# Attention's value products for two query blocks at a time, and the last down products in PSUM banks of their own

## The chip, the core and the metric

The kernel runs on one core of a Trainium2 chip. Five engines work side by side and meet only through semaphores: TensorE (PE in the profile, with its weight loads shown apart as PEld), VectorE (DVE), ScalarE (ACT), GpSimd (POOL) and SyncE (SP), which here issues nearly all DMA transfers. [...] The metric is the device time of one launch in microseconds; less is better. A time is given as the median of several runs.

## The reference

The reference is one transformer block in fp32 over 1024 tokens of width 1024, one batch row, one layer:

```
mod = silu(c) @ w_ada + b_ada            # sh1 sc1 g1 sh2 sc2 g2
h = rmsnorm(x) * (1 + sc1) + sh1
q_a k_a v_a | q_d k_d v_d z b a = split(h @ w_in)
y_attn  = dilated attention, 8 heads of 64, softmax over three dilated branches
y_delta = gated delta rule, 8 heads of 64, chunks of 64, short convolution
x = x + g1 * (concat(y_attn, y_delta) @ w_out)
h = rmsnorm(x) * (1 + sc2) + sh2
x = x + g2 * ((silu(h @ w_gate) * (h @ w_up)) @ w_down)      # d_ff = 2816
out = rmsnorm(x) * final_norm_g
```

The three dilated branches are one causal softmax over all 1024 keys: a bias table holds the log of how many branches contain a distance, and distances in no branch are masked.

## The kernel before

**Precision.** Products that need fp32 accuracy are made of three fp32r products: each operand is cut into a high part (an ACT cast) and a low part (a DVE or POOL subtraction), and high x high, high x low, low x high are summed in one PSUM bank. Attention's transposes (`L1332`) and value products (`L1349`) are plain fp32 instead; TensorE executes each plain fp32 value product as two recorded matmuls with a weight load each.

**Order of the work.** The build function writes the program in one order. A list scheduler then fixes the order on each engine: it plays the program against modelled durations and gives a free engine the ready instruction of the highest priority. Priority is the place in the program; `urgent()` moves what it encloses 6000 places forward, which in attention and in the down products is ahead of everything else in sight. `tc.issue_after(ins)` makes what it encloses follow `ins` on that engine. A tile of a pool with `bufs=n` waits until one of n buffers has been released by its last reader. `FILL` and `ahead()` place filler products (`L590`: input projections, later products with `w_out`) between the small products of delta rule and attention.

**Attention (`attend`, about 495 to 670 us).** A unit is one pair of heads `hp` (4 of them) and one block `qb` of 128 queries (8 of them). At step i of 32 units the program holds the scores of unit i (`att_score`: S products on PE, a DVE reduction to X, an ACT exponential, a POOL scaling), the transposes of unit i-1 (`att_turn`: per head one or two banks of up to four 128x128 transposes, copied by ACT for the first four key blocks and by DVE for the rest into a tile `et`), and the value products of unit i-3 (`att_value`). There are 4 `et` buffers, two per unit. `att_value` runs over the key blocks kb = 0..qb and in each over both heads e; head e takes 64 columns of `va` as weights, so its product uses half the columns of the PE array and lands in half the partitions of one bank `y`. Four query blocks share that bank, one after another; after the fourth, ACT copies it (`yh`, L1360) and DVE takes the rest (`yl`, L1361). A unit has 2(qb+1) value products.

**Down products (`down`, from 1186 us to the end).** The FFN's second half is done by a seven-product (Strassen-like) scheme: token half l, output half s, seven passes i over f = 0..10. Per f, two tiles of 128x512 are loaded by SP (`raw_load`: `da` activations, `db` weights; 6 buffers `wr`), cut by ACT and DVE (`parts`, 5 buffers each for `wh` and `wl`, urgent), and used in 12 matmuls: four token blocks b, each into a bank of its own, three products each. Passes 0, 1, 4 and 6 sum in the four banks X, pass 2 in Y, passes 3 and 5 in Z (Y's banks). After a pass its four banks are finished by `ends`, which the next pass calls at f = 1, 3, 5, 7: a copy, or `sum_end`: add, multiply by g2, add x, an ACT square whose accumulator gives the row sum; a row that is complete goes through `row_out`: an add, a square root, a reciprocal, two scalings and two stores.

The last pass (`down(6, ..., final=True)`) multiplies f = 0..6 for all four blocks, and keeps the parts of f = 7..10 (TAIL = 4) in 8 extra buffers; then each block b gets its 12 last products and is finished at once, so that only block 3 is left at the end:

```python
            if final:
                for f in range(n, NF):
                    down_mm(bank, b, pr[f], f, first)
                with urgent():
                    final[b]()
```

There `final[b]()` is L1835 (bank times g2), L1836 (plus x), L1838 (square), L1844 (sum of the two halves), L1845 (root), L1846 (reciprocal), L1851 on ACT and L1853 on DVE (the two halves scaled), L1856 (stores).

## Time and profile before

| | |
|---|---|
| time, median of 3 runs | 1403.61 us (1403.61 to 1405.59) |
| the profiled execution's own time | 1406.77 us |
| its span, first to last instruction | 1404.7 us |
| PE busy | 1349.1 us, 96% |
| DVE / ACT / POOL busy | 876.6 / 662.6 / 287.1 us |
| granted TensorE clock, mean | 0.992 |
| DMA moved | 245.68 MB, mean 175 GB/s |

In a list of instructions in order of time, a row is: start, duration, engine, line, operation, what is written from what, shape, and how many equal neighbours are merged (x32); a bracket at its end tells idle time before it and what ended that. Matmuls are pipelined: a 128x512 matmul is shown 0.39 us long, but the next starts 0.23 us later. In a table of stretches, each engine has its busy time and in brackets its number of instructions, then come the clock, the DMA engines' busy share and GB/s. A row of a group has minimum, median and maximum duration in ns.

### The profile page before, as it was taken

Reading aid. Unit: us, or ns where it says so; the run is one execution under the profiler, and the core shown is the slowest. Engines: PE = TensorE matmul, PEld = TensorE weight load, DVE = VectorE, ACT = ScalarE, POOL = GpSimd, SP = SyncE. Lnnn points to the kernel's source line nnn. Section 1 sums busy time; section 2 is a strip of 40 time slices with the busy share of each in tenths; the row PEclk is TensorE's granted clock in tenths of the full one; section 3 lists DMA queues with packets and bytes.
Section 4 is the critical chain, followed back from the end, with each engine's and each line's share of the span. In section 5 each row is a group of like instructions: output and inputs, shape, how many; then the busy total and the mean of one; then the engine's idle time right before and its main releaser. Section 6 shows DMA issues by size and latency. Waiting matters only on the chain.

```text
span 1404.7 us, 24467 instructions
## 1 busy us (share of the span) xinstructions
PE 1349.1 (96%) x8984; PEld 1110.7 (79%) x8984; DVE 876.6 (62%) x1669; ACT 662.6 (47%) x1287; POOL 287.1 (20%) x267
## 2 busy tenths in 40 slices
PE   8998999998999899999999999999999999999997
PEld 4778877887888677777877878888888888888886
DVE  3688484556835433666228987667575776474487
ACT  4498424356234355766147733333333333444446
POOL 2346412344213344543162000000000000000000
PEclk9999999999999999999999999999999999999999
DMA  8666565486352445521584345545363665765566
GB/s 307 229 190 167 162 209 167 130 248 180 119 151 68 129 128 169 184 91 54 169 263 161 120 158 169 175 147 176 130 207 106 210 207 186 259 222 197 194 221 238
DMA packets 169872, 245.68 MB, mean 175 GB/s; under 512 B 32566, under 2 KB 73831, under 8 KB 169752
## 3 DMA queue, kind: packets, MB, share of 16 engines
q1 hardware_dynamic: 169752, 244.12, 53.8%
q8 instruction: 71, 1.16, 0.3%
q14 instruction: 49, 0.40, 0.1%
HBM read 181.30 MB, written 67.48 MB: 177 GB/s over the span
## 4 chain that ended last, share of the span: by engine, by line
PE 56%; DMA 4%; DVE 3%; ACT 2%; issue 1%; POOL 1%; SPq 0%; DVEq 0%; ACTq 0%; POOLq 0%
PE wua L1591 9%; PE wga L1591 8%; PE X L1786 6%; PE wuc L1591 4%; PE wgc L1591 4%; PE Z L1786 4%; PE g_a L590 3%; PE wo L590 3%; PE y L1349 3%; PE wgb L1591 2%; PE Y L1786 2%; PE wub L1591 2%; PE tr L1332 2%; PE S L1308 1%; PE S L1309 1%
## 5 line engine op out<-in xcount | busy, mean ns | idle before, releaser
L1581 DVE TENSOR_TENSOR wl_db<-wr_db,wh_db 128x512 fp32r<-128x512 f32 x77 | 53.1, 691 | 74.7 <-ACT wh_db L1580 74.6
L1580 ACT CAST wh_db<-wr_db 128x512 fp32r<-128x512 f32 x77 | 47.9, 622 | 96.5 <-PE X L1786 41.3
L1312 DVE CUSTOM_DVE_ANT_0 X<-S,ng 128x512 f32<-128x512 f32 (+3 forms) x64 | 36.8, 586 | 55.4 <-PE S L1309 39.8
L1786 PE MATMUL X<-wh_db,wl_da 128*128 128x512 f32 x176 | 68.5, 389 | 0.0
L1786 PE MATMUL X<-wh_db,wh_da 128*128 128x512 f32 x176 | 68.5, 389 | 0.0
L1786 PE MATMUL X<-wl_db,wh_da 128*128 128x512 f32 x176 | 68.5, 389 | 0.0
L1317 ACT ACTIVATE X<-X,sc 128x128 f32<-128x128 f32 (+7 forms) x64 | 49.4, 773 | 36.9 <-DVE sc L1312 33.5
L1319 POOL TENSOR_SCALAR X<-X,sc 128x128 f32<-128x128 f32 (+7 forms) x64 | 50.5, 792 | 75.1 <-DVE sc L1318 70.7
L1581 DVE TENSOR_TENSOR wl_da<-wr_da,wh_da 128x512 fp32r<-128x512 f32 x77 | 52.8, 685 | 2.0 <-ACT wh_da L1580 2.0
L590 PE MATMUL g_a<-hh,wh_a 128*128 128x512 f32 x128 | 53.1, 415 | 0.0
L590 PE MATMUL wo<-yh,wh_wo 128*128 128x512 f32 x128 | 51.6, 406 | 1.0 <-DVE xo L1400 1.0
L590 PE MATMUL wo<-yl,wh_wo 128*128 128x512 f32 x128 | 50.6, 395 | 0.9 <-DVE yl L1411 0.9
L590 PE MATMUL g_a<-hh,wl_a 128*128 128x512 f32 x128 | 51.2, 400 | 0.0
L590 PE MATMUL wo<-yh,wl_wo 128*128 128x512 f32 x128 | 51.2, 400 | 0.0
L590 PE MATMUL g_a<-hl,wh_a 128*128 128x512 f32 x128 | 51.1, 399 | 0.0
L1580 ACT CAST wh_da<-wr_da 128x512 fp32r<-128x512 f32 x77 | 47.4, 616 | 6.8 <-PE wua L1591 5.8
L1580 ACT CAST wh_wg_s<-wg_s 128x512 fp32r<-128x512 f32 x33 | 20.6, 623 | 57.3 <-PE wuc L1591 24.6
L1332 PE MATMUL tr<-ident,X 128*128 128x128 f32 x288 | 44.7, 280 | 2.8 <-DVE et L1335 1.7
L231 POOL TENSOR_TENSOR wl_wo<-wr_wo,wh_wo 128x512 fp32r<-128x512 f32 x24 | 32.9, 1375 | 61.2 <-ACT wh_wo L230 55.9
L1349 PE MATMUL y<-et,va 128*64 128x128 f32 x576 | 43.5, 281 | 0.3 <-DVE yl L1361 0.3
L1332 PEld LDWEIGHTS tr<-ident,X 128*128 128x128 f32 x288 | 34.0, 142 | 12.2 <-issue 4.3
L1580 ACT CAST wh_wu_s<-wu_s 128x512 fp32r<-128x512 f32 x33 | 20.4, 621 | 43.8 <-PE wga L1591 17.2
(544 smaller groups left out, 4324.2 us busy)
## 6 DMA issues: line engine op xcount, KB each, us to landing
wm<-in_wada SPq DMA_DIRECT2D x44, 512.0 KB, 6.6
wr_da<-ao_d SPq DMA_DIRECT2D x77, 256.0 KB, 3.0
wr_wu<-in_wu SPq DMA_DIRECT2D x50, 256.0 KB, 2.7
wr_wg<-in_wg SPq DMA_DIRECT2D x48, 256.0 KB, 2.8
ao_d<-a SPq DMA_DIRECT2D x44, 256.0 KB, 2.5
wr_wd<-in_wdn SPq DMA_DIRECT2D x44, 256.0 KB, 3.1
wr_db<-wt_d SPq DMA_DIRECT2D x44, 256.0 KB, 2.7
ao_d<-as SPq DMA_DIRECT2D x33, 256.0 KB, 2.0
```

Source lines behind the costliest of these rows:

```text
L231: (eng or nc.gpsimd).tensor_tensor(out=lo[:, :n], in0=raw[:, :n], in1=hi[:, :n].bitcast(F32), op=ALU.subtract)
L590: last[0] = nc.tensor.matmul(ps, a[:, w0], b[k0 + k4][:, cs], start=(i == 0), stop=(i == n - 1))
L1308: nc.tensor.matmul(ps[:, 0 : c1 - c0], QS[:, qs], KS[:, c0:c1], start=True, stop=False)
L1312: nc.vector.tensor_tensor_reduce(out=X[:, c0:c1], in0=ps[:, 0 : c1 - c0], in1=ng[:, u + c0 : u + c1], scale=1.0, scalar=(3e38 if m is None ...
L1317: nc.scalar.activation(X[:, 0:nk], X[:, 0:nk], AF.Exp, scale=-1.0, bias=m, accum_out=sc[:, 2:3])
L1319: nc.gpsimd.tensor_scalar(out=X[:, 0:nk], in0=X[:, 0:nk], scalar1=sc[:, 3:4], scalar2=0.0, op0=ALU.mult, op1=ALU.add)
L1332: nc.tensor.transpose(ps[:, (kb - c0) * P : (kb - c0 + 1) * P], X[:, kb * P : kb * P + P], ident)
L1349: nc.tensor.matmul(yps[64 * e : 64 * e + 64, yc], va[:, kb, 64 * e : 64 * e + 64], ets[e][:, kb, :], start=(kb == 0), stop=(kb == qb),)
L1580: nc.scalar.copy(hi, src)
L1581: (eng or nc.vector).tensor_tensor(out=lo, in0=src, in1=hi.bitcast(F32), op=ALU.subtract)
L1591: nc.tensor.matmul(ps, a[:, w0], b, start=(first and k == 0 and n_ == 0), stop=(k == 3 and n_ == 2), skip_group_check=True,)
L1786: nc.tensor.matmul(bank[b], a[:, ts_], w, start=(first and f == 0 and n_ == 0), stop=(f == NF - 1 and n_ == 2), skip_group_check=True,)
```

## The change

In attention, `att_value` is called for odd `qb` only, and does the products of qb and qb-1 together. They are urgent, and ordered: first two products of head 1 of block qb (for qb < 7 with key blocks 0 and qb, for 7 with 7 and 0), then, after the second of these on PE, all the others. The bank `y` is taken at the first of the two groups. The `et` buffers go from 4 to 6.

In the down products, the tiles of f = 7..10 of the last pass are loaded and cut during pass 5 (at f = 1, 3, 5, 7), their weights first multiplied by g2 on DVE; their products go into four banks W of their own (Z's banks, free after pass 5's ends). So X of the last pass is complete after f = 6, and `last_end` does X times g2 plus x while the W products run; per block there is then one add, the square and `row_out`. In `row_out` the sum of the two halves is no longer an instruction: the square is scaled to give means, eps is added to the first half's mean where that half is finished, and the root takes that sum as its bias.

```diff
-XB, ETB, AT, AV = 5, 4, 1, 3
+XB, ETB, AT, AV = 5, 6, 1, 3
...
-        if qb % 4 == 0:
+        if qb % 4 == 1:
             ybanks[hp] = ybank(f"y{hp}_{qb}")
         yps = ybanks[hp]
...
+        seq = {q: (0, *range(q, 0, -1)) if q < 7 else (q, *range(q)) for q in (qb - 1, qb)}
+        parts = [(q, kb, e) for q in (qb, qb - 1) for kb in seq[q] for e in (1, 0)]
+        parts[1:2], parts[2:3] = parts[2:3], parts[1:2]
+        mm = None
+        with turn(f"y{hp}_{qb}"), urgent():
+            for i, (q, kb, e) in enumerate(parts):
+                with tc.issue_after(mm.ins) if i else ExitStack():
+                    ins = nc.tensor.matmul(
+                        yps[64 * e : 64 * e + 64, (q % 4) * P : (q % 4 + 1) * P],
+                        va[:, kb, 64 * e : 64 * e + 64], ets[q % 2][e][:, kb, :],
+                        start=(kb == seq[q][0]), stop=(kb == seq[q][-1]),
                     )
+                mm = ins if i < 2 else mm
...
-            if i >= AV:
+            if i >= AV and units[i - AV][1] % 2:
                 hp, qb = units[i - AV]
-                att_value(hp, qb, ets.pop(i - AV))
+                att_value(hp, qb, [ets.pop(i - AV - 1), ets.pop(i - AV)])
...
         b = raw_load(wdn_src(i, f), f"db{i}_{f}")
+        if p is not None:
+            with urgent():
+                nc.vector.tensor_tensor(out=b, in0=b, in1=g2r[:, dsl[0]], op=ALU.mult)
         return parts(a, f"da{i}_{f}", p=p), parts(b, f"db{i}_{f}", p=p)
...
-        n = NF - TAIL if final else NF
-        for f in range(NF):
-            pr[f] = down_parts(i, f, pz if f >= n else None)
...
+        n = NF - TAIL if tail else NF
+        for f in range(n):
+            pr[f] = down_parts(i, f)
+            for b in range(4):
+                down_mm(bank, b, pr[f], f, first and f == 0, f == n - 1)
+            if i == 5 and f % 2 == 1 and len(held) < TAIL:
+                t = NF - TAIL + len(held)
+                held[t] = down_parts(6, t, pz)
             if f % 2 == 1 and ends:
                 ends.pop(0)()
...
-                    down_mm(bank, b, pr[f], f, first)
+                    down_mm(tail, b, held[f], f, f == n, f == NF - 1)
                 with urgent():
-                    final[b]()
+                    last[b]()
...
-        sq = pz.tile([P, HALF], F32, name=f"sq3_{l}{s}{b}", tag="sq3", bufs=2)
-        nc.scalar.activation(sq, t, AF.Square, accum_out=rn[:, 4 * l + b, s : s + 1])
+        square(l, s, b, t)
         if s == l:
+            r = rn[:, 4 * l + b]
+            nc.vector.tensor_tensor(out=r[:, 2:3], in0=r[:, s : s + 1], in1=eps1, op=ALU.add)
...
-        nc.vector.tensor_tensor(out=r[:, 2:3], in0=r[:, 0:1], in1=r[:, 1:2], op=ALU.add)
-        nc.scalar.activation(r[:, 2:3], r[:, 2:3], AF.Sqrt, bias=eps1, scale=1.0 / D)
-        nc.vector.reciprocal(r[:, 3:4], r[:, 2:3])
+        nc.scalar.activation(r[:, 3:4], r[:, 1 - l : 2 - l], AF.Sqrt, bias=r[:, 2:3])
+        nc.vector.reciprocal(r[:, 3:4], r[:, 3:4])
...
+    def last_end(src, more):
+
+        def at(b):
+            x = x_in(1, 0, b)
+            t = y[1, 0][b]
+            nc.vector.tensor_tensor(out=t, in0=src[b], in1=g2r[:, dsl[0]], op=ALU.mult)
+            nc.vector.tensor_tensor(out=t, in0=t, in1=x, op=ALU.add)
+
+            def go():
+                nc.vector.tensor_tensor(out=t, in0=more[b], in1=t, op=ALU.add)
+                square(1, 0, b, t)
+                row_out(1, b)
...
-    down(6, X, False, sum_end(1, 0, X, None, True), final=True)
+    W = four("W")
+    down(6, X, False, last_end(X, W), tail=W)
```

More of the change, by code (lines that the diff above doesn't have):

```diff
@@ L1341, in att_value @@
         va = loaded[hp][0]
-        if qb % 4 == 0:
+        if qb % 4 == 1:
             ybanks[hp] = ybank(f"y{hp}_{qb}")
         yps = ybanks[hp]
-        yc = slice((qb % 4) * P, (qb % 4 + 1) * P)
-        with turn(f"y{hp}_{qb}"):
-            for kb in range(qb + 1):
-                for e in range(2):
-                    nc.tensor.matmul(
-                        yps[64 * e : 64 * e + 64, yc], va[:, kb, 64 * e : 64 * e + 64], ets[e][:, kb, :],
-                        start=(kb == 0), stop=(kb == qb),
+        seq = {q: (0, *range(q, 0, -1)) if q < 7 else (q, *range(q)) for q in (qb - 1, qb)}
[9 more added lines that the diff above has]
+                        start=(kb == seq[q][0]), stop=(kb == seq[q][-1]),
                     )
+                mm = ins if i < 2 else mm
         if qb % 4 == 3:
@@ L1770, in build @@
     nc.sync.dma_start(gfr, I["gfin"].to_broadcast([P, D]))
+    dsl = [slice(s * HALF, (s + 1) * HALF) for s in range(2)]
     def wdn_src(i, f):
@@ L1779, in down_parts, with down_mm @@
         b = raw_load(wdn_src(i, f), f"db{i}_{f}")
+        if p is not None:
+            with urgent():
+                nc.vector.tensor_tensor(out=b, in0=b, in1=g2r[:, dsl[0]], op=ALU.mult)
         return parts(a, f"da{i}_{f}", p=p), parts(b, f"db{i}_{f}", p=p)
-    def down_mm(bank, b, pr, f, first):
+    def down_mm(bank, b, pr, f, first, last):
         (ah, al_), (wh, wl) = pr
@@ L1786, in down_mm, with down @@
             nc.tensor.matmul(
-                bank[b], a[:, ts_], w, start=(first and f == 0 and n_ == 0), stop=(f == NF - 1 and n_ == 2),
-                skip_group_check=True,
+                bank[b], a[:, ts_], w, start=(first and n_ == 0), stop=(last and n_ == 2), skip_group_check=True,
             )
     ends = []
-    def down(i, bank, first, end, final=False):
+    held = {}
+    def down(i, bank, first, end, tail=None):
         pr = {}
-        n = NF - TAIL if final else NF
-        for f in range(NF):
-            pr[f] = down_parts(i, f, pz if f >= n else None)
-            if f < n:
-                for b in range(4):
-                    down_mm(bank, b, pr[f], f, first)
+        n = NF - TAIL if tail else NF
[6 more added lines that the diff above has]
+                held[t] = down_parts(6, t, pz)
             if f % 2 == 1 and ends:
                 ends.pop(0)()
-        assert not ends
-        if final:
+        while ends:
+            ends.pop(0)()
+        if tail:
             with urgent():
-                final = [end(b) for b in range(4)]
+                last = [end(b) for b in range(4)]
         for b in range(4):
-            if final:
+            if tail:
                 for f in range(n, NF):
-                    down_mm(bank, b, pr[f], f, first)
+                    down_mm(tail, b, held[f], f, f == n, f == NF - 1)
                 with urgent():
-                    final[b]()
+                    last[b]()
             else:
@@ L1824, in build @@
     rn = pz.tile([P, 8, 4], F32, name="rn", tag="rn")
-    dsl = [slice(s * HALF, (s + 1) * HALF) for s in range(2)]
-    xr = {}
     def x_in(l, s, b):
@@ L1831, in x_in, with square @@
         return x
+    def square(l, s, b, t):
+        sq = pz.tile([P, HALF], F32, name=f"sq3_{l}{s}{b}", tag="sq3", bufs=2)
+        nc.scalar.activation(sq, t, AF.Square, scale=1.0 / 32, accum_out=rn[:, 4 * l + b, s : s + 1])
     def half_end(l, s, b, src, t, x):
@@ L1856, in row_out @@
             nc.sync.dma_start(out[tb * P : (tb + 1) * P, dsl[s]], t)
+    def last_end(src, more):
[8 more added lines that the diff above has]
+                row_out(1, b)
+            return go
+        return at
     def copy_end(dst, src):
@@ L1868, in go @@
                 t = y[l, s][b]
-                if other is not None:
-                    add(t, src[b], other[b])
-                half_end(l, s, b, src[b] if other is None else t, t, x)
+                add(t, src[b], other[b])
+                half_end(l, s, b, t, t, x)
                 if row:
```

## The prediction

> **What bounds the kernel now.** I read the page first (busy shares), then tables of stretches around the two places that change, then PE's instructions in order of time there, then what PE waited for in attention, and last the end of the DVE and ACT lists.

> ```profile
> span 1404.7 us, 24467 instructions
> PE 1349.1 (96%) x8984; PEld 1110.7 (79%) x8984; DVE 876.6 (62%) x1669; ACT 662.6 (47%) x1287; POOL 287.1 (20%) x267
> ...
> 573.00:637.00 64.00, 60.68 (x478) 46.71 (x477) 45.14 (x135) 44.28 (x94) 31.63 (x30) 0.97 0.40 126
> ...
> 1336.08:1357.84 21.76, 21.76 (x97) 18.02 (x97) 18.75 (x31) 11.62 (x25) 0.00 (x0) 1.00 0.74 242
> 1357.84:1366.00 8.16, 8.16 (x37) 6.76 (x37) 4.85 (x8) 3.43 (x7) 0.00 (x0) 1.00 0.62 186
> 1366.00:1396.00 30.00, 29.92 (x132) 24.43 (x131) 26.29 (x53) 21.50 (x44) 0.00 (x0) 1.00 0.72 251
> ```

> PE is the bound: 96% over the whole, 95% in the middle of attention (60.68 of 64.00 us), without a gap in the last two down passes. In the stretches the columns after the length are PE, PEld, DVE, ACT, POOL, clock, DMA share, GB/s. Whatever PE needs less in attention the whole program ends earlier, since the products behind wait for PE too; after PE's last matmul only the end chain counts.

> **Attention: what one group of value products costs.** PE's list between 498.84 and 669.28 us holds 45 unbroken groups of `y` products where 32 units ask for 32; the first and last, and five stretches that give prices:

> ```profile
> 498.84 0.44 PE L1349 MATMUL y<-et,va 128*64 128x128 f32 x4
> ...
> 609.21 0.40 PE L1308 MATMUL S<-KS,QS 128*128 128x512 f32 x1
> 609.44 0.39 PE L1309 MATMUL S<-KL,QS 128*128 128x512 f32 x1
> 609.76 0.43 PE L1349 MATMUL y<-et,va 128*64 128x128 f32 x2
> 610.12 0.39 PE L1308 MATMUL S<-KS,QS 128*128 128x256 f32 x1
> ...
> 637.31 1.97 PE L1349 MATMUL y<-et,va 128*64 128x128 f32 x32
> 639.21 0.50 PE L1308 MATMUL S<-KS,QS 128*128 128x512 f32 x1
> 639.55 0.40 PE L1309 MATMUL S<-KL,QS 128*128 128x512 f32 x1
> 639.78 0.39 PE L1308 MATMUL S<-KS,QS 128*128 128x512 f32 x1
> ...
> 641.50 0.44 PE L1349 MATMUL y<-et,va 128*64 128x128 f32 x4
> 641.86 0.33 PE L1308 MATMUL S<-KS,QS 128*128 128x128 f32 x1
> ...
> 666.29 3.05 PE L1349 MATMUL y<-et,va 128*64 128x128 f32 x50
> ```

> From start to the next start: 32 records take 1.90 us, 4 take 0.36, so 0.055 a record and 0.14 fixed. Before a group, S to `y` takes 0.32 where S to S takes 0.23: 0.09. After it, S to S takes 0.34 (639.21 to 639.55) where the next takes 0.23: 0.11. A group costs 0.34 us beside its records. Two records (one product) take 0.36, as long as four: a product without a partner in the other half of the array loses 0.10, and 18 of the 45 groups have an odd number of products.

> The change asks for 16 groups. Their first products wait for the head whose copies come last, and the rest follows, so they should stay whole. Step by step:
> - 29 groups fewer at 0.34: -9.9 us; 18 odd ends at 0.10: -1.8.
> - The new head of a group puts two products of head 1 and then two of head 0 in a row, so pairs in opposite halves begin two records late: two steps of 0.11 (two records each), 0.22 us. Bounds 0 and 0.22; I take 0.22, since the lone two records above were not filled up either: 16 x 0.22 = +3.5.
> - For qb = 5 the first two products wait for two different copies (ACT's and DVE's). If the first goes alone, four groups split: 4 x 0.34 = +1.4; bounds 0 and 1.4, and I take 1.4, because the x2 group above is just such a lone first product.
> - `et` from 4 to 6 buffers, `y`'s bank taken one unit later, the filler 0.64 of `y0_0` without a taker: nothing on PE. The cover is that PE has S, transposes or filler to do; if it is gone, the copies' wait below is what PE sees.
> Sum: -6.8 us; ends -11.7 (no loss at the head, no split) and -1.0 (half the groups broken up as now).

> [...]

> What could now wait is the head of each group: it is urgent, so it stands in PE's order as soon as the planned copy ends, and everything behind it on PE (S, transposes, filler) waits with it.

> ```profile
> PE tr L1332 <- DVE et L1335: 1.7, 3, 0.8
> PE y L1349 <- DVE yl L1361: 0.3, 1, 0.3
> ...
> L1337 ACT COPY et<-tr x60: 267/565/606, 500.4 to 666.0; 128x512 f32<-128x512 f32 x40, 128x384 f32<-128x384 f32 x8, 128x128 f32<-128x128 f32 x6, 128x256 f32<-128x256 f32 x6
> ```

> These are PE's waits (total us, times, longest) and the copy. `y` waited once, for its bank, and never for a copy, though the broken groups show that products were often placed right at a copy's end. Bounds 0 and one copy, 0.565, per group (9.0 us). I take 0.

> **Down: what moves into pass 5.** For four f: 8 loads of 256 KB by SP, 8 casts on ACT, 8 subtractions and 4 new multiplications on DVE, from pass 6 into the first eight f of pass 5. DVE's price is 18.75 us / 31 = 0.605 each, so 12 x 0.605 = 7.3 us. The first eight f then ask DVE for 26.0 us in 21.76. Of it only subtractions and held work are urgent: 28 x 0.605 = 16.9 us, which fits. The 16 steps of pass 4's ends (9.7 us) get 4.8 there and need 4.9 in the last three f, where six subtractions of 8.16 us leave 4.5: they end 0.4 us into pass 6. Block 3's bank X, which an end must have read, is wanted 3 x 0.68 = 2.0 us into pass 6 (three blocks of three matmuls at 0.227). So PE doesn't wait, with 1.6 us to spare.

> The loads: 22 of pass 5, 4 of `x`, 8 moved; 28 fall into the first eight f, 7.3 MB in 21.8 us.

> ```profile
> 1344.24:1346.96 2.72, 2.72 (x13) 2.25 (x13) 2.72 (x5) 1.21 (x3) 0.00 (x0) 1.00 0.85 257
> ...
> 1379.50:1382.20 2.70, 2.70 (x14) 2.23 (x13) 2.70 (x6) 2.68 (x6) 0.00 (x0) 1.00 0.94 335
> ```

> At the first row's rate (257/0.85 = 302 GB/s when full) they take 24.3 us, 2.5 too long; at the second's (356 GB/s) 20.6, in time. SP sends them in order through the 6 `wr` buffers, and a late held tile stops the DVE and ACT work queued behind it. In these rows DVE was full and PE lost nothing, with three f of loads in hand. Bounds 0 and +2.5; I take +0.3, nearer to the row that shows the same pile-up in pass 6. [...]

> In pass 6, DVE loses 8 x 0.605 of its 26.29 us. The banks W are free when pass 5's ends have read Z, more than 10 us before PE asks for them. Eight tiny additions of eps go into passes 2 and 4, under their matmuls. PE's 924 matmuls stay.

> **The end.** Now, for block 3, DVE and ACT:

> ```profile
> 1395.54 0.39 PE L1786 MATMUL X<-wh_db,wl_da 128*128 128x512 f32 x1
> ...
> 1386.66 0.68 DVE L1836 TENSOR_TENSOR y<-y,xr 128x512 f32<-128x512 f32 x1
> 1388.92 0.75 DVE L1853 SCALAR_TENSOR_TENSOR y<-y,rn,gfr 128x512 f32<-128x512 f32 x1
> ...
> 1396.64 0.68 DVE L1835 TENSOR_TENSOR y<-X,g2r 128x512 f32<-128x512 f32 x1
> 1397.65 0.69 DVE L1836 TENSOR_TENSOR y<-y,xr 128x512 f32<-128x512 f32 x1
> 1399.19 0.16 DVE L1844 TENSOR_TENSOR rn<-rn 128x1 f32<-128x1 f32 x1
> 1400.19 0.75 DVE L1853 SCALAR_TENSOR_TENSOR y<-y,rn,gfr 128x512 f32<-128x512 f32 x1
> ```

> PE ends at 1395.93. The last scaling starts 4.26 us later, behind a multiplication, an addition, root and reciprocal that are also mixed with block 2's. The row of an undisturbed block (addition 1386.66, scaling 1388.92) needs 2.26 us from addition to scaling. After the change one addition is left in front and L1844's step is gone. With it at 1396.0 the scaling starts by 1398.3 at the latest undisturbed (-1.9), or 0.6 later behind block 2's scaling; without L1844, 0.3 earlier. So -1.9, ends -1.3 and -2.2. The stores behind keep their 3.8 us to 1404.7.

> **Sum.** -6.8 + 0.3 - 1.9 = -8.4 us. The profiled execution has a span of 1404.7 and a time of 1406.77; it becomes 1396.3 and 1398.4. The median of the runs is 1403.61, so 1395.2.

> **Rivals.**
> - *Slower: each group waits at its head.* Place: PE before the 16 groups. Price: a copy of 0.565 and about 0.2 of hand-over (my estimate from the gaps of the end chain, 0.2 to 0.4 between engines), 0.77 x 16 = 12.2 us: 1407.4. It decides from 8.4/16 = 0.53 us per group. For: urgent leaves no slack, and S, transposes and filler stand behind it. Against: `y` waited 0.3 us in all. Chance 0.14.
> - *Pass 5 starves.* If PE waits for all the DVE work, 26.0 - 21.76 = 4.2 us: 1399.1. For: the sum is over 100%. Against: full DVE slices with PE at 2.72 of 2.72. Chance 0.09.
> - *PE saves, and then waits for the chain of scores.* In 573 to 637 us stand 24 of the 45 groups; ACT and DVE are busy 44 and 45 of 64 us there, and little filler is at hand. If half of the attention saving turns into idle PE, 1403.6 - 3.4 - 1.6 = 1398.6. Chance 0.15.
> - *The groups stay broken up.* Then only the end gains, and -1.0 at most in attention: 1401 to 1402, within 0.2%. For: readiness, not the program, broke them until now. Against: the order after the second product. Chance 0.13.

> **How the numbers follow.** The forecast has the rest, 0.49, and a range of its own of 1390 to 1397.5 (-11.7 and -2.2 with no loss in pass 5 is 1389.7; a loss of 2.5 in pass 5 in place of 0.3 gives 1397.4). The range of 8 in 10 goes from 1390.5 to 1403.0: it leaves out the slower rival (0.14) and a little below. Faster by over 0.2% (2.8 us, about what the three runs, 1403.61 to 1405.59, can tell from no change): 0.49 + 0.09 + 0.15 = 0.73; within: 0.13; slower: 0.14.

> **What the profile after would show.** Sixteen to twenty groups of `y`, of 12, 28, 44 and 60 records, the longest about 3.6 us; PE's waits for `et` near zero; attention's last group earlier by about 7 us; pass 5 at 29.9 us of PE without a gap; between PE's end and the last scaling 2.4 us in place of 4.3. The prediction is wrong if PE waits for ACT or DVE copies before the groups by over 0.5 us each, if pass 5 shows PE gaps after DVE or a load, or if PE's idle time in attention grows by what the groups save.

## The result, and the profile after

The changed kernel takes 1400.38 us (median) beside 1404.78 us for the kernel before in the same session: a ratio of 0.9963 with a 95% interval of 0.9949 to 0.9976, that is 5.2 us less (3.4 to 7.2). Run once more beside other kernels it gave 0.9975 (0.9961 to 0.9988). So it is faster, as forecast, by some 40 to 60% of the 8.4 us of the forecast.

The head of the page after, and a table of stretches of the changed kernel. Columns after the length are as in the prediction: PE, PEld, DVE, ACT, POOL, clock, DMA share, GB/s. The first row is the middle of attention, the second and third are pass 5 of the down products, the last is pass 6.

```profile
span 1397.3 us, 24428 instructions
PE 1343.9 (96%) x8984; PEld 1109.9 (79%) x8984; DVE 878.8 (63%) x1677; ACT 661.4 (47%) x1287; POOL 283.6 (20%) x267
```

```profile
572.00:636.00 64.00, 59.58 (x512) 47.80 (x511) 47.68 (x150) 48.45 (x107) 30.90 (x33) 0.97 0.46 128
1327.82:1349.60 21.78, 21.50 (x93) 16.90 (x93) 19.70 (x34) 12.88 (x25) 0.00 (x0) 1.00 0.82 260
1349.60:1359.00 9.40, 8.38 (x37) 6.59 (x36) 8.61 (x18) 5.36 (x12) 0.00 (x0) 1.00 0.87 274
1359.00:1391.00 32.00, 31.42 (x138) 25.25 (x136) 28.22 (x52) 19.50 (x42) 0.00 (x0) 1.00 0.62 208
```

PE has the same 8984 instructions and 5.2 us less busy time (1349.1 to 1343.9). In attention it does 512 records in 64 us where it did 478, with less busy time (59.58 us against 60.68). In pass 5, where it had no gap before, it now has 93 matmuls in 21.78 us where 97 went into 21.76: four matmuls of 0.227 us are missing there, and more behind. So one half of the change gained and the other half lost, and the two are read apart below.

**Attention.** PE's list in order of time: a group of 44 and of 60 records under filler work, and a group of 44 at a lower granted clock (0.63; see the table further down).

```profile
523.76 0.39 PE L590 MATMUL g_a<-hh,wh_a 128*128 128x512 f32 x1
524.08 2.63 PE L1353 MATMUL y<-et,va 128*64 128x128 f32 x44
526.64 0.50 PE L590 MATMUL g_a<-hl,wh_a 128*128 128x512 f32 x1
...
541.17 0.39 PE L590 MATMUL g_a<-hh,wl_a 128*128 128x512 f32 x1
541.49 3.50 PE L1353 MATMUL y<-et,va 128*64 128x128 f32 x60
544.93 0.50 PE L590 MATMUL g_a<-hh,wh_a 128*128 128x512 f32 x1
545.26 0.39 PE L590 MATMUL g_a<-hl,wh_a 128*128 128x512 f32 x1
...
586.74 4.02 PE L1353 MATMUL y<-et,va 128*64 128x128 f32 x44
```

There are exactly sixteen groups, four each of 12, 28, 44 and 60 records. From start to the next start 44 records take 2.56 us and 60 take 3.44, again 0.055 a record and 0.15 fixed. The fixed part is what it was before, so the order of heads at the front of a group adds nothing, and no group is split at qb = 5. PE's waits in attention (480 to 680 us; total, times, longest) name no copy in front of `y`:

```profile
PE tr L1332 <- POOL X L1319: 2.4, 3, 1.0
PE S L1308 <- DVE sc L1312: 2.0, 5, 1.1
PE wo L590 <- DVE yl L1416: 1.9, 1, 1.9
PE tr L1332 <- DVE et L1335: 1.9, 3, 0.9
```

**Pass 5.** PE's list, the DMA issues of SP (they begin with SPq), DVE and ACT at the two places where PE stood; in brackets the idle time ahead of an instruction and what ended it.

```profile
1350.47 0.40 PE L1796 MATMUL Z<-wh_db,wh_da 128*128 128x512 f32 x1
1351.89 0.50 PE L1796 MATMUL Z<-wl_db,wh_da 128*128 128x512 f32 x1 [1.02 <-DVE wl_db L1586]
```

```profile
1336.73 0.32 SPq L1577 DMA_DIRECT2D wr_db<-wt_d  x1
...
1338.54 0.32 SPq L1577 DMA_DIRECT2D wr_da<-ao_d  x1
1342.14 0.33 SPq L1577 DMA_DIRECT2D wr_db<-in_wdn  x1
...
1344.02 0.32 SPq L1577 DMA_DIRECT2D wr_da<-ao_d  x1
```

```profile
1339.03 0.69 DVE L1605 TENSOR_TENSOR y<-X,r 128x512 f32<-128x512 f32 x1
1340.82 0.69 DVE L1789 TENSOR_TENSOR wr_db<-wr_db,g2r 128x512 f32<-128x512 f32 x1 [1.10 <-DMA wr_db<-wt_d]
1341.43 0.68 DVE L1586 TENSOR_TENSOR wl_db<-wr_db,wh_db 128x512 fp32r<-128x512 f32 x1
...
1349.27 0.69 DVE L1586 TENSOR_TENSOR wl_da<-wr_da,wh_da 128x512 fp32r<-128x512 f32 x1 [0.88 <-ACT wh_da L1585]
```

```profile
1348.62 0.62 ACT L1585 CAST wh_da<-wr_da 128x512 fp32r<-128x512 f32 x1 [1.01 <-DMA wr_da<-ao_d]
```

SP's waits for a buffer (1318 to 1356 us; total, times, longest):

```profile
SPq L1577 <- DVE wl_db L1586: 15.5, 17, 3.2
```

The held weights' multiplication (L1789) stands in DVE's queue with its load, issued at 1336.73, not yet landed: DVE idles 1.10 us, with the subtractions of pass 5 queued behind. No load goes out between 1338.54 and 1342.14: SP's longest wait, 3.2 us, lies there, and it ends with one of those subtractions (1341.43), which releases a `wr` buffer. The load issued at 1344.02 lets ACT start its cast only at 1348.62, 4.6 us later; DVE waits 0.88 us for that cast, and PE then waits 1.02 us for the subtraction. Over passes 5 and 6 the start-to-start intervals that exceed the usual 0.227 us by more than 0.05 add up to 2.8 us, 1.2 of it at 1351.89; 2.3 us lie in pass 5 and the rest in pass 6.

**The end.** PE's last matmul and DVE's last two instructions on block 3 (the addition and the scaling):

```profile
1390.34 0.39 PE L1796 MATMUL W<-wh_db,wl_da 128*128 128x512 f32 x1
...
1390.77 0.69 DVE L1883 TENSOR_TENSOR y<-W,y 128x512 f32<-128x512 f32 x1
...
1392.78 0.75 DVE L1869 SCALAR_TENSOR_TENSOR y<-y,rn,gfr 128x512 f32<-128x512 f32 x1
```

PE ends at 1390.73 and the last scaling starts 2.05 us later, where it was 4.26 us; from PE's end to the end of the span it is 6.6 us (1397.3) where it was 8.8 (1404.7).

### The profile page after: what moved, and what is told of

Its sections match the earlier page's. It is cut to its first block, busy times and chain, and to the rows that moved or that the text cites. A ratio compares the mean times of both kernels' runs of the same rounds, so it can differ in the third digit from the quotient of the medians.

```text
span 1397.3 us, 24428 instructions
## 1 busy us (share of the span) xinstructions
PE 1343.9 (96%) x8984; PEld 1109.9 (79%) x8984; DVE 878.8 (63%) x1677; ACT 661.4 (47%) x1287; POOL 283.6 (20%) x267
## 4 chain that ended last, share of the span: by engine, by line
PE 53%; DVE 5%; DMA 3%; issue 2%; ACT 2%; POOL 1%; SPq 0%; DVEq 0%; ACTq 0%; POOLq 0%
PE wua L1596 9%; PE wga L1596 8%; PE X L1796 6%; PE wuc L1596 4%; PE wgc L1596 4%; PE wo L590 4%; PE g_a L590 3%; PE wgb L1596 2%; PE Z L1796 2%; PE Y L1796 2%; PE wub L1596 2%; PE y L1353 2%; PE tr L1332 2%; PE S L1308 1%; PE S L1309 1%
## 5 line engine op out<-in xcount | busy, mean ns | idle before, releaser
L1796 PE MATMUL X<-wl_db,wh_da 128*128 128x512 f32 x160 | 62.4, 390 | 0.3 <-DVE wl_db L1586 0.3
L1796 PE MATMUL X<-wh_db,wl_da 128*128 128x512 f32 x160 | 62.3, 389 | 0.0
L1796 PE MATMUL X<-wh_db,wh_da 128*128 128x512 f32 x160 | 62.3, 389 | 0.0
L1317 ACT ACTIVATE X<-X,sc 128x128 f32<-128x128 f32 (+7 forms) x64 | 49.5, 775 | 24.3 <-DVE sc L1312 22.7
L1332 PE MATMUL tr<-ident,X 128*128 128x128 f32 x288 | 45.8, 278 | 5.1 <-POOL X L1319 2.4
L1332 PEld LDWEIGHTS tr<-ident,X 128*128 128x128 f32 x288 | 32.8, 140 | 17.0 <-POOL X L1319 6.2
L1585 ACT CAST wh_wg<-wr_wg 128x512 fp32r<-128x512 f32 x31 | 19.2, 622 | 46.3 <-PE wua L1596 18.9
```

Source lines behind the costliest of these rows:

```text
L1317: nc.scalar.activation(X[:, 0:nk], X[:, 0:nk], AF.Exp, scale=-1.0, bias=m, accum_out=sc[:, 2:3])
L1332: nc.tensor.transpose(ps[:, (kb - c0) * P : (kb - c0 + 1) * P], X[:, kb * P : kb * P + P], ident)
L1585: nc.scalar.copy(hi, src)
L1796: nc.tensor.matmul(bank[b], a[:, ts_], w, start=(first and n_ == 0), stop=(last and n_ == 2), skip_group_check=True,)
```

## The experiments

**The two halves apart.** `e1_att` has the new attention with the old down products, `e2_down` the reverse.

```diff
 e1_att: att_value as changed; down, down_parts, row_out and the ends as before
 e2_down: down, down_parts, row_out and the ends as changed; in attention
-XB, ETB, AT, AV = 5, 6, 1, 3
+XB, ETB, AT, AV = 5, 4, 1, 3
```

> Attention's part alone, down products as before. The two traces say: from the first score product to the last product with w_out 6.8 us less, nothing else. If that holds: 0.5% faster than before (ratio about 0.995), 16 value groups, no gap in pass 5. If the whole gain of the change (5 us) is made up of both parts with the sign that the forecast gave them, attention alone gives only 3 us (0.998). If the down part costs more than it brings, attention alone is faster than the whole change (below 0.9963).

> The down part alone, attention as before. Theory: the end chain is 2.2 us shorter, PE's gaps in passes 5 and 6 cost 2.5 to 3.1 us, so between 0.3 and 0.9 us slower in the profile and no difference that can be measured (0.999 to 1.002). Forecast's sizes (gap 0.3, end 1.9): 1.6 us faster (0.9989).

Measured, as ratios to the kernel before, which ran beside each on the same chip, with their intervals, here and below: `e1_att` 0.9948 (0.9928 to 0.9968), which is 7.3 us less (4.5 to 10.1); `e2_down` 0.9996 (0.9979 to 1.0013), 0.6 us less (3.0 less to 1.8 more). The gain is that of attention. The down half is worth nothing that can be measured: its shorter end (6.5 us behind PE in this profile too) is paid back in passes 5 and 6, where the intervals add up to 3.4 us of lost PE time in `e2_down`. The two halves sum to 7.9 us, and the whole gave 5.2 and 3.5 in two sessions; the intervals hold that difference.

The price of a group can be read from these profiles. This table is worked out from PE's records between the first score product `S` and the last `wo` product: the sum of start to next start, less idle time, by kind, in us. `e6_single`, `e7_plain` and `e8_heads` are described further down, `f1_change` is the changed kernel again.

```
              groups    y     tr     S    y+tr+S   idle   whole stage
before          45    40.5   34.0   40.4   114.9   12.6      282.2
e2_down         45    40.3   33.4   40.4   114.1   15.2      288.7
changed         16    35.4   29.0   41.3   105.7   13.4      275.3
f1_change       16    35.2   29.4   41.4   106.0   15.8      279.7
e1_att          16    35.2   29.1   41.1   105.4   13.4      276.8
e6_single       30    36.9   29.8   41.6   108.4   14.2      280.2
e7_plain        53    45.0   30.5   41.5   117.0   14.7      291.7
e8_heads        16    60.0   29.5   41.1   130.6   12.0      300.4
```

The steadiest column is y+tr+S: 114.1 to 114.9 for the old groups and 105.4 to 106.0 for the new ones, 8.8 us apart. Part of its spread is the clock. For stretches of 3.4 us and more the granted clock is 0.5 (in the changed kernel's attention from 586.23 to 589.64 us), and groups of `y` that fell into one took longer: the group of 44 at 586.74 took 3.96 us from start to next start in place of 2.56. In the profile of `e5_pool` (further down), whose attention is that of the changed kernel, two groups of 60 took 5.03 and 5.99 us in place of 3.43, and the column is 109.3. If the records in such stretches are counted as long as the same records elsewhere in their profile, the column is about 114 for the old groups and 104 to 105 for the new ones (eight profiles), some 9.6 us apart. Idle time and filler differ by some 3 us between profiles of the same attention code (the changed kernel's stage took 275.3 and 279.7), so the length of one stage in one profile says little.

**Whole groups, but of one query block.** Is it the pairing or the wholeness that pays?

```diff
-        if qb % 4 == 1:
+        if qb % 4 == 0:
...
-        seq = {q: (0, *range(q, 0, -1)) if q < 7 else (q, *range(q)) for q in (qb - 1, qb)}
-        parts = [(q, kb, e) for q in (qb, qb - 1) for kb in seq[q] for e in (1, 0)]
-        parts[1:2], parts[2:3] = parts[2:3], parts[1:2]
+        seq = {q: (0, *range(q, 0, -1)) if q < 7 else (q, *range(q)) for q in (qb,)}
+        parts = [(q, kb, e) for q in (qb,) for kb in seq[q] for e in (1, 0)]
+        if qb:
+            parts[1:2], parts[2:3] = parts[2:3], parts[1:2]
...
-            if i >= AV and units[i - AV][1] % 2:
+            if i >= AV:
```

> As the changed kernel, but each group holds the products of one query block alone, with the same order of heads and urgent: 32 whole groups in place of 16. If each group has a price of its own of 0.24 us (6.8 us saved over 29 groups): 3.8 us more than the changed kernel, ratio to before 0.998 to 1.000. If it is only the breaking up that costs: within 1 us of the changed kernel, ratio 0.995 to 0.997. If the price is 0.34 as I forecast: 5.4 us more, ratio about 1.000.

Measured: 0.9975 (0.9957 to 0.9993), between the two forecasts, so the time doesn't decide. The records do: 30 unbroken stretches of `y` (three units were split, others met), and y+tr+S at 108.4 us. As the profiles stand, some 6.1 of the 8.8 us come from going from 45 broken groups to 30 nearly whole ones, and 2.7 from 30 to 16, 0.19 us a group. But in the one profile of `e6_single` no stretch of lower clock falls into attention; with those of the others taken out as above, it is 5.6 and some 4 us (0.29 a group). Either way the larger part is that groups stay whole, and the pairing adds the smaller; how much smaller is not settled.

**Paired, but in plain order.** What keeps a group whole?

```diff
-        seq = {q: (0, *range(q, 0, -1)) if q < 7 else (q, *range(q)) for q in (qb - 1, qb)}
-        parts = [(q, kb, e) for q in (qb, qb - 1) for kb in seq[q] for e in (1, 0)]
-        parts[1:2], parts[2:3] = parts[2:3], parts[1:2]
+        seq = {q: tuple(range(q + 1)) for q in (qb - 1, qb)}
+        parts = [(q, kb, e) for q in (qb - 1, qb) for kb in seq[q] for e in (0, 1)]
...
-                with tc.issue_after(mm.ins) if i else ExitStack():
+                with ExitStack():
```

> As the changed kernel, two query blocks in a group and urgent, but the products stand in plain order (block qb-1 first, kb rising, heads in turn) and none is told to come behind another. If it is the order with the late head first that keeps a group whole: 24 to 40 groups, and half or more of the 6.8 us of attention is lost, ratio 0.998 to 1.001. If the groups are whole because all their copies are done by the time they are placed: 16 to 20 groups, ratio 0.995 to 0.998.

Measured: 1.0049 (1.0026 to 1.0072), slower than the kernel before by about 7 us, and worse than either expectation. PE's list, rows of `y` and their neighbours, and PE's waits for `y` in 480 to 680 us:

```profile
573.55 0.43 PE L1352 MATMUL y<-et,va 128*64 128x128 f32 x2
573.91 0.50 PE L590 MATMUL g_a<-hl,wh_a 128*128 128x512 f32 x1
574.35 0.87 PE L1352 MATMUL y<-et,va 128*64 128x128 f32 x10
...
579.70 0.43 PE L1352 MATMUL y<-et,va 128*64 128x128 f32 x2 [0.18 <-ACT et L1337]
```

```profile
PE y L1352 <- ACT et L1337: 4.8, 4, 2.7
```

There are 53 groups, 21 of them a lone product (x2), and PE waits 4.8 us at the head of groups for ACT's copies. By the program the first product takes head 0, whose copies come first; that it goes off alone and its partner follows when head 1's copy is there fits these rows. These are two of the prediction's rivals at once, broken groups and a wait at the head: pairing and urgency alone bring them about. The edit takes out two things, the order with the late head first and the rule that the rest follows the second product; together they keep the rivals away, and they were not tried apart.

**All products of head 1 first.** How far does PE draw a partner forward? In the changed kernel the queue of a group holds two products of head 1, then two of head 0, and so on in turn; each product is two records (576 for 288 products).

```diff
-        parts = [(q, kb, e) for q in (qb, qb - 1) for kb in seq[q] for e in (1, 0)]
-        parts[1:2], parts[2:3] = parts[2:3], parts[1:2]
+        parts = [(q, kb, e) for e in (1, 0) for q in (qb, qb - 1) for kb in seq[q]]
...
-                mm = ins if i < 2 else mm
+                mm = ins
```

> As the changed kernel, but in each group all products of head 1 stand in PE's order first and all of head 0 behind them. If PE starts matmuls strictly in order, nothing runs beside its partner: 0.109 us a record, 6.6 us for a group of 60, and 576 x 0.055 = 31 us more in all, about 1431 us. If it draws the partner forward however far back it stands: 3.4 us for 60, time as the changed kernel. If it looks only some way ahead: between, and the length of the run of lone records at the head shows how far.

Measured, in two runs: 1.0136 (1.0100 to 1.0173), 19 us more than before. The group of 60 in PE's list:

```profile
607.61 6.38 PE L1352 MATMUL y<-et,va 128*64 128x128 f32 x60
```

The starts of the records in ns from the start of the group, here and in the changed kernel's group at 628.79 us:

```
changed, records 0-7:      0   14  160  174  270  283  379  392
e8_heads, records 0-4:     0  160  269  378  487
e8_heads, records 25-36:  2780 2889 2895 2998 3055 3107 3164 3217 3273 3382 3492 3601
```

In `e8_heads` the records start 0.109 us apart up to the 27th (the first two 0.160). The first record of the other half starts 6 ns behind the 27th, when three of the thirty records of head 1 still have to start; then the two halves run side by side until head 1 is through, and head 0 runs alone. In the changed kernel the partner has to pass exactly three records (the second of the first product and two of the second product), and it starts 14 ns behind the first record of all (13 to 14 ns in each of the sixteen groups). So in both kernels the partner was drawn forward past three records and, with more ahead of it, no further; which record belongs to which head is inferred from the halves, since the trace names no head.

**Pass 5: load or DVE.** `e3_hold4` moves all the held work one pass forward, into pass 4. `e4_own` moves only the loads: into eight buffers of their own and ahead, while the DVE and ACT work on them stays in pass 5 (but for one cast, at 1207.32 us), each piece of it behind the subtraction that the program wrote last before it.

```diff
 e3_hold4:
-            if i == 5 and f % 2 == 1 and len(held) < TAIL:
+            if i == 4 and f % 2 == 1 and len(held) < TAIL:
 e4_own:
+    def held_load(f):
+        for n_, src in (("da", _.ao[6][f]), ("db", wdn_src(6, f))):
+            t = pz.tile([P, HALF], F32, name=f"hr_{n_}{f}", tag="hr", bufs=2 * TAIL)
+            nc.sync.dma_start(t, src)
+            hraw[n_, f] = t
...
+            with tc.issue_after(lastsub[0].ins), urgent():
                 nc.vector.tensor_tensor(out=b, in0=b, in1=g2r[:, dsl[0]], op=ALU.mult)
...
+            if i == 4 and f % 2 == 1 and f // 2 < TAIL:
+                held_load(NF - TAIL + f // 2)
```

> The whole change with the four held f loaded and cut in pass 4 in place of pass 5. Pass 4 has DVE at 15.2 of 29.9 us and DMA at 0.59, so both theories of the gaps (late loads, full DVE) expect none here: PE's gaps of 2.5 us gone, the end still 6.6 us after PE's last matmul, about 2.5 us faster than the change as it is (ratio to before about 0.9945). If the gaps only move into pass 4, the time stays.

> The whole change, but the held tiles are loaded during pass 4 into eight buffers of their own, so that they neither take wr buffers nor can be late; DVE's and ACT's work on them stays in pass 5, each behind a subtraction of that pass. Late loads as the cause: no gap in pass 5, as fast as with the held work in pass 4 (0.9945). Full DVE as the cause: the gaps of about 2.5 us stay, time as the change (0.9963).

Measured: `e3_hold4` 0.9925 (0.9903 to 0.9947), `e4_own` 0.9927 (0.9908 to 0.9946); the loads of `e4_own` went out at 1202.8 to 1216.9 us, well ahead of pass 5, since their buffers were free. Pass 5 of `e4_own`:

```profile
1331.00:1352.80 21.80, 21.80 (x97) 18.05 (x97) 21.80 (x39) 14.04 (x27) 0.00 (x0) 1.00 0.66 213
```

DVE is busy for 21.80 of 21.80 us and PE has no gap. A full DVE is therefore not what stopped PE in pass 5. That leaves the loads, or the place of the held work in DVE's queue, which this edit changes too.

**Pass 5: the held work on POOL.** The opposite cut: DVE is relieved and the loads stay.

```diff
-                nc.vector.tensor_tensor(out=b, in0=b, in1=g2r[:, dsl[0]], op=ALU.mult)
-        return parts(a, f"da{i}_{f}", p=p), parts(b, f"db{i}_{f}", p=p)
+                nc.gpsimd.tensor_tensor(out=b, in0=b, in1=g2r[:, dsl[0]], op=ALU.mult)
+        e = None if p is None else nc.gpsimd
+        return parts(a, f"da{i}_{f}", eng=e, p=p), parts(b, f"db{i}_{f}", eng=e, p=p)
```

> As the changed kernel, but the held tiles' 4 multiplications and 8 subtractions are given to POOL, so DVE loses 12 x 0.605 = 7.3 us of the first eight f of pass 5; their loads stay where they are. If DVE, asked for 26.0 us in 21.76, is what stopped PE (my rival 2): no start-to-start interval over 0.6 us is left in passes 5 and 6, PE's matmuls end 2.5 to 3 us earlier against the first X matmul, ratio 0.992 to 0.994. If late loads stopped it: 2 to 3.5 us of intervals over 0.28 us stay in passes 5 and 6, and the ratio stays at 0.995 to 0.998.

Measured: 1.0010 (0.9988 to 1.0032), so the edit cost about what the change had gained. PE's waits in passes 5 and 6, then DVE's and POOL's lists:

```profile
PE Z L1797 <- DVE wl_db L1586: 6.0, 5, 1.8
PE Z L1797 <- ACT wh_db L1585: 1.1, 1, 1.1
```

```profile
1330.05 1.37 DVE L1586 TENSOR_TENSOR wl_db<-wr_db,wh_db 128x512 fp32r<-128x512 f32 x1 [2.80 <-ACT wh_db L1585]
1331.34 1.77 DVE L1586 TENSOR_TENSOR wl_da<-wr_da,wh_da 128x512 fp32r<-128x512 f32 x1
...
1335.67 0.68 DVE L1586 TENSOR_TENSOR wl_da<-wr_da,wh_da 128x512 fp32r<-128x512 f32 x1
```

```profile
1329.58 1.30 POOL L1586 TENSOR_TENSOR wl_da<-wr_da,wh_da 128x512 fp32r<-128x512 f32 x1 [574.18 <-PE X L1797]
1330.83 1.74 POOL L1789 TENSOR_TENSOR wr_db<-wr_db,g2r 128x512 f32<-128x512 f32 x1
```

Gaps stayed, but grew to 7.1 us of waits (9.4 us of longer intervals, counted as above), so this run says less than it was meant to: POOL took 1.29 to 1.79 us for what DVE did in 0.68, and DVE's own subtraction beside it took 1.37 and 1.77 in place of 0.68. Every held tile stays longer in its `wr` buffer, and the loads behind it wait for that buffer: of SP's waits in 1325 to 1366 us, 15.5 us end with one of POOL's subtractions. DVE's queue holds no held work here, and PE stops all the same. So the run agrees with the loads as the cause, and adds a second effect of its own.

**Pass 5: the ring or the queue.** A late load can mean that eight more transfers crowd the queue, or that the held tiles occupy the ring of six `wr` buffers. `e9_own5` has the held tiles' loads at the very place in SP's queue where the changed kernel has them, but in the eight buffers of `e4_own`.

```diff
 against e4_own:
-            nc.sync.dma_start(t, src)
+            with tc.issue_after(lastload[0].ins), urgent():
+                nc.sync.dma_start(t, src)
...
-            if i == 4 and f % 2 == 1 and f // 2 < TAIL:
+            if i == 5 and f % 2 == 1 and f // 2 < TAIL:
```

> As e4_own, but the loads of the held tiles stand in SP's queue exactly where the changed kernel has them, in pass 5; only their buffers are their own eight, so the six wr buffers serve pass 5's tiles alone. If the held tiles' time in the ring of six is what makes pass 5's next loads late: less than 0.5 us of intervals over 0.28 us beyond the usual 0.227 in passes 5 and 6, ratio 0.992 to 0.994. If it is the eight more loads in those 22 us that make everything behind them in the queue late: 2 to 3.5 us stay, ratio 0.995 to 0.998.

Measured: 0.9952 (0.9929 to 0.9974), a ratio whose interval holds both expectations; the profile decides. Of `e9_own5`: a stretch of pass 5; the issue of one held tile in SP's list and its first use in DVE's; the grouped issues of the held weights in 1318 to 1356 us (count, KB each, median us to landing). Then the grouped line of the changed kernel that holds them, with two of pass 6:

```profile
1328.89:1350.69 21.80, 21.80 (x97) 17.93 (x96) 21.80 (x40) 14.24 (x27) 0.00 (x0) 1.00 0.86 278
```

```profile
1335.27 0.42 SPq L1794 DMA_DIRECT2D hr_db<-wt_d  x1
```

```profile
1342.19 0.68 DVE L1801 TENSOR_TENSOR hr_db<-hr_db,g2r 128x512 f32<-128x512 f32 x1
```

```profile
hr_db<-wt_d SPq DMA_DIRECT2D x4, 256.0 KB, 4.5
```

```profile
wr_db<-wt_d SPq DMA_DIRECT2D x6, 256.0 KB, 3.5
```

No interval over 0.24 us is left in passes 5 and 6, though DVE is full, the DMA share is higher than in the changed kernel (0.86 against 0.82), and loads take longer to land (medians of 3.5 to 4.5 us by group, against 3.0 to 3.5; for the held weights each of the two lines above rests on the one load whose landing the trace tells). The tile loaded at 1335.27 is used 6.9 us later; in the changed kernel the one loaded at 1336.73 was wanted 3.0 us later (1339.03 and 0.69) and used after 4.1. What was missing, by these figures, is the lead: six buffers at two tiles per f of 2.72 us give 6 x 2.72 / 2 = 8.2 us from the issue of a load to its tile's release; with the held tiles in the same ring it is 24 tiles in eight f, 3 per f (the tiles of `x` have buffers of their own), and 6 x 2.72 / 3 = 5.4 us, of which a load alone takes 3.5 to 4.6. One thing is not separated: `e9_own5` also has the held DVE work behind that pass's subtractions, as `e4_own` has. For the tile compared here, counted from the first matmul of pass 5 (1328.89 us, 1327.65 in the changed kernel), the load went out at 6.4 us in place of 9.1, and the weight was wanted at 13.3 in place of 12.1: of the 3.9 us more lead 2.7 come from the earlier load and 1.2 from the later place in DVE's queue.

**Side by side.** The changed kernel and `e3_hold4` once more, on one chip.

> The changed kernel once more, beside f2_hold4 on one chip, for a second profile of the same program. If the ring of six buffers is what costs PE time: again 2 to 3.5 us of intervals over 0.28 us in passes 5 and 6, at about the same products. The three times of PE that the groups change (y, transposes, scores) come to 105 to 106 us again, against 114.8 before; filler and idle time in attention may differ by 2 us from the first profile.

> The held tiles loaded and cut in pass 4 once more, beside f1_change on one chip. If the ring is the cause: no interval over 0.3 us in passes 5 and 6, and 2 to 4 us less than f1_change, which the ratios should show as 0.0015 to 0.003 apart. If the gap between the two in the earlier runs came from the chip: the same ratio within 0.001.

Measured: `f1_change` 1402.04 us, 0.9975 (0.9961 to 0.9988); `f2_hold4` 1398.33 us, 0.9948 (0.9927 to 0.9968). They are 3.7 us apart. The second profile of the changed kernel has its largest gap at the same kind of place:

```profile
1353.13 0.50 PE L1796 MATMUL Z<-wh_db,wh_da 128*128 128x512 f32 x1
1354.69 0.50 PE L1796 MATMUL Z<-wl_db,wh_da 128*128 128x512 f32 x1 [1.06 <-DVE wl_db L1586]
```

The table of stretches of 60 us of passes 5 and 6, first `f1_change`, then `e3_hold4`:

```profile
1331.00:1391.00 60.00, 58.56 (x253) 46.82 (x252) 54.76 (x99) 35.90 (x73) 0.00 (x0) 1.00 0.71 240
```

```profile
1330.00:1390.00 60.00, 60.00 (x266) 49.68 (x265) 49.52 (x90) 33.22 (x69) 0.00 (x0) 1.00 0.64 212
```

253 matmuls against 266: 13 x 0.227 = 3.0 us. With the held tiles cut a pass earlier the kernel beats both the changed one and the one before, by 0.5 to 0.75% against the latter.

## Why the prediction was right or wrong

- **Direction and place: right.** Faster, by attention; the end gained too, but passes 5 and 6 took that back. PE is the bound, and what it needs less there ends the program earlier.
- **Attention, -6.8: about right as a sum, wrong in three of its terms.** By itself it measured -7.3 (-4.5 to -10.1). The 29 groups at 0.34 and 18 odd ends at 0.10 were put at -11.7; PE's time in products, transposes and scores fell by 8.8. In the first pair of profiles the products themselves fell by 5.1 (40.5 to 35.4), where 29 x 0.14 + 1.8 = 5.9 had been put; transposes and scores, a group's neighbours, by 4.1 (74.4 to 70.3), where 29 x 0.20 = 5.8 had. With the stretches of lower clock taken out as above, the products fell by 6.3 and the neighbours by 3.4: the price of the products was about right, that of the neighbours was too high. It was read beside scores alone; why it came out lower is not settled, since filler, which is not in this sum, varies by more than that. The terms +3.5 (order of heads) and +1.4 (splits at qb = 5) did not come at all. Two errors cancelled.
- **The order of heads, +3.5: wrong.** I took the upper bound, from a lone x2 group that was not filled up. But no partner stood behind that product in the queue, so the row could not show what happens when one does. No group of the changed kernel shows the 0.22: in all sixteen the partner in the opposite half of the array starts 13 to 14 ns behind the first record, past three records queued ahead of it; in the group of `e8_heads` above it also passed three.
- **No wait at the heads: right.** The waits name no copy in front of `y`. (That PE's waits for `et` would go near zero did not come: transposes still wait for it, 1.7 us before and 1.9 after.) That this rival was real, and what held it off, `e7_plain` shows: in plain order PE waited there 4.8 us, and the kernel came out slower.
- **Pass 5, +0.3: the term that failed.** Over passes 5 and 6 it measured 2.8 us in both profiles of the changed kernel (2.3 and 2.1 of it in pass 5) and 3.4 in `e2_down` (2.7 in pass 5). The part in pass 6 may not be the held tiles': the old down products in `e1_att` show 0.8 there, though the kernel before shows none. The sign that the prediction named for being wrong here, gaps of PE in pass 5 after DVE or a load, came. The bound was +2.5, and I went for the row of pass 6 at 0.94 DMA share. The sentence that was wrong is "with three f of loads in hand": three f is what six buffers hold at two tiles per f; with the held tiles it is three tiles per f, and six buffers hold two f. The price was derived from the transfer rate, by which the loads were late by 2.5 us or not at all; the rate was not the cause, as `e9_own5` shows at a higher share (0.86 and 278 GB/s without a gap, against 0.82 and 260). That the ring was the cause, and not the place of the held work in DVE's queue, is argued from SP's waits, `e5_pool` and the lead, not tried by itself.
- **Pass 5, DVE: right that it fits.** The rival in which PE starves for DVE named 1399.1 us, close to what came, but its mechanism is not the one: `e4_own` and `e9_own5` run with DVE full and without a gap.
- **PE saves and then waits for the scores: not shown.** Idle time in the stage was 12.6 and 15.2 us with the old attention and 13.4 to 15.8 with the new. One wait did grow, that of `wo` for `yl`, from 0.9 to 1.9 us.
- **The end, -1.9: right.** The profile has -2.2 from PE's end to the end of the span, the bound that I named without L1844.
- **The sum.** With 2.8 in the place of 0.3 the forecast would have been -5.9, against -5.2 (-3.4 to -7.2) and -3.5 (-1.7 to -5.5). Taken from the forecast's 1403.61, 5.2 us less is 1398.4: inside the wide range, but outside the 1390 to 1397.5 that the forecast gave its own mechanism. That attention's term came so close is luck, since two errors cancelled in it.

## What to carry to other kernels

When work is moved ahead into a stage, count not only each engine's time there but also the lead that a shared ring of buffers still gives each load: buffers over tiles per unit of time, beside the landing time under load. Here an urgent group of products stayed whole when its first product waited for the operand that comes last and the rest followed the second product; the same group in plain order broke into three times as many pieces and made the kernel slower. A price taken from a row holds only if that row had the chance to behave otherwise.

## What the runs showed that I had not expected

```profile
585.17 0.51 PE L590 MATMUL wo<-yl,wh_wo 128*128 128x512 f32 x1 [1.92 <-DVE yl L1416]
```

```profile
586.74:590.70 3.96, 3.96 (x46) 3.79 (x45) 1.76 (x7) 2.99 (x5) 3.96 (x3) 0.63 0.88 217
```

A pause of 1.8 to 1.9 us stands at this place in all nine profiles with sixteen groups. In six of them the granted clock falls to 0.5 within 1.3 us behind it; in `f1_change`, `e4_own` and `e5_pool` it falls only some 12 us later, and there the group of 44 keeps its 2.56 us. Whether the pause causes the lower clock was not tried.
